# A two-layer hybrid decoder trunk on one NeuronCore: halved first weights, warm-up products, a shorter last norm, paired outputs, and a planner with longer notices

## The chip, the cores and the metric

The kernel runs on one core of a Trainium2 chip. The metric is the device time of one execution in microseconds (us). TensorE (PE) multiplies; a product is a weight load (PEld) and a stream of columns (a matmul) into a PSUM bank. VectorE (DVE), ScalarE (ACT) and GpSimd (POOL) do the rest; SyncE (SP) issues almost all DMAs.

## The reference

Input x is 1 x 1024 x 1024 in float32. Each of the two layers normalises, projects into four mixers, normalises each mixer's output, projects back and adds; then it runs a SwiGLU feed-forward network (FFN) with an inner width of 2816 and adds. A final norm ends it.

```python
for l in range(DEPTH):
    h = rmsnorm(x, attn_norm[l])
    proj = h @ w_in[l]
    ...
    y_a = mla_attention(...)          # latent attention, rotary keys, causal
    y_b = short_gated_conv(...)
    y_c = multiscale_pool(...)
    y_d = swa_sink_attention(...)     # sliding window of 128
    ...
    x = x + mixed @ w_o[l]
    h2 = rmsnorm(x, ffn_norm[l])
    gate, up = jnp.split(h2 @ w_gate_up[l], 2, axis=-1)
    x = x + (jax.nn.silu(gate) * up) @ w_down[l]
return rmsnorm(x, final_norm)
```

`rmsnorm` is x / sqrt(mean(x^2) + 1e-6) times a gain.

## The kernel before

*Layout.* x is held transposed: eight tiles of 128 features (`NK`), each in two halves t = 0, 1 of 512 positions (`HT`). All products run in fp32r, three per pair of tiles (`mm3`, L272): weights and activations are split into a rounded part `hi` and a remainder `lo`, and hi*hi, hi*lo and lo*hi are summed in PSUM. So every weight tile costs ACT a copy (L215 for the projections, L283 elsewhere) and DVE a subtraction (L216, L284), and every x tile that enters costs a gain copy on ACT (`act.activation(hi, f, AF.Copy, scale=gain)`, L286) and a subtraction on DVE (L287). The 2x2 block products of the FFN go through a Strassen-like scheme of seven products; the sums of the down weights that it needs are made on GpSimd (`dn_sums`, L161) and written to DRAM (`qd`).

*The start.* `par` (gains and other small constants, 128 x 86) is loaded on GpSimd's queue (L131), everything else on SP's. The first weights of the projections come through `weights` (L207: load of 128 x 1024; L215 copy; L216 subtraction), the x tiles through `enter` (L366), and their squares for the first norm through `SumSq.add` (L313 for the first square, L318 and L324 for a further square and its addition). The first products are those of the key weights with half 0 of x. `ones` is a 128 x 128 tile of ones, written by DVE at the start; a product with it sums over the partitions.

*The norm.* `SumSq.add` squares a tile on ACT and adds it to a running sum on DVE; the last addition also adds the epsilon (L320). `rnorm` multiplies the sum with `ones` (L336, in float32; L333 where the sum is split first), takes a logarithm and an exponential on ACT (L338, L339), refines the result (L340, L341, L344) and leaves 1/rms.

*The end.* In the last layer the last of the seven products of the down projection (`B22`) is done for columns 0 to 255 of half 1 first, then for 256 to 511: for each of four m, products into a bank, `evac` (L1575: adds the bank to x on DVE), squares. After the fourth, `rnorm(1, cols, tag="s")` and `finish`: for each of eight tiles one DVE instruction, x times gain times 1/rms (L380), and one output DMA of 128 x 256 (128 KB, L384). The output of half 0 leaves in 256 KB tiles.

*The order.* The program is recorded first; `order_engines` then sets the order of instructions on each engine. `steps_of` makes a step of each instruction with an estimated length; `arrange` runs a list schedule: each engine takes, of the steps whose inputs have arrived, the one with the smallest place. A place is the step's rank in the recorded program plus a number from the table `MOVES`, keyed by group (the neighbouring steps of one engine on one tile). `SIGNAL[a][b]` is the notice that engine b needs after a step of engine a ends; a PSUM bank or temporary may be taken anew 40 ns after its last use. In the trace each line number of a helper (L272, L283) stands for all its callers.

Of the kernel before, what the change touches and what calls it, by code (L numbers as in the profile page):

```python
# [18 lines left out]
P = 128  # L19
# [92 lines left out]
def trunk_kernel(ctx: ExitStack, tc: tile.TileContext, ins, out):  # L112
# [17 lines left out]
    par = cpool.tile([P, L * PC_N + NK], F32, name="par")  # L130
    pool.dma_start(par, ins["params"])  # L131
# [50 lines left out]

    def tmp(tag="te"):
        return tpool.tile([P, HT], F32, name=tag, tag=tag, bufs={"te": 2, "tn": 3, "tp": 3}[tag])
# [18 lines left out]
    def weights(src, n):  # L203
        if n > 2 * P:
            s = F.pair()
            raw = F.ap2(s)
            sp.dma_start(raw[:, :n], src)  # L207
# [7 lines left out]
        act.copy(hi[:, :n], raw[:, :n])  # L215
        dve.tensor_tensor(out=lo[:, :n], in0=raw[:, :n], in1=rd(hi[:, :n]), op=ALU.subtract)  # L216
# [20 lines left out]
    def expect_layer(l):  # L237
        for m in (2, 3, 0, 4, 5, 6, 1, 13, 14, 10, 11, 12, None, 7, 8, 9):
            if m is None:
                expect(rope_weights, l)  # L240
            else:
                expect(weights, ins["w_in"][l, m], 2 * HT)
        for d in range(NK):
            expect(weights, ins["w_o"][l, d, :, 2 * P :], 6 * P)
# [53 lines left out]
    class SumSq:  # L298
# [7 lines left out]
        def add(self, t, f, cols=whole):  # L306
# [12 lines left out]
            if m == self.n // P:  # L319
# [6 lines left out]
        def rnorm(self, t, cols=whole, tag="t", parts=False):  # L326
# [8 lines left out]
            else:  # L335
                pe.matmul(p, ones, a, start=True, stop=True)  # L336
# [24 lines left out]

    def enter(t):

        for k in range(NK):
            s = xf[k][t] = F.half()
            sp.dma_start(F.ap(s), x_in[k, :, t * HT : (t + 1) * HT])  # L366
            hh[k][t] = half_split(F.ap(s), pcol(0, PC_ATTN + k))

    def enter_norm(t):
# [3 lines left out]
        ratt[t] = ss.rnorm(t, parts=True)  # L373

# [10 lines left out]

    last_silu = None
    for l in range(L):
# [1251 lines left out]
        for cols in (slice(0, 256), slice(256, HT)) if last else ():  # L1639
            for m, p, w in tail:  # L1640
# [6 lines left out]
                ss.add(1, F.ap(x[2 * m][1])[:, cols], cols)  # L1647
            ratt[1] = ss.rnorm(1, cols, tag="s")
            finish(x, 1, cols)
# [6 lines left out]
    "DVE": {"PE": 55, "DVE": 33, "ACT": 33, "POOL": 79, "SP": 27},  # L1656
    "ACT": {"PE": 52, "DVE": 33, "ACT": 25, "POOL": 77, "SP": 26},
    "POOL": {"PE": 79, "DVE": 33, "ACT": 32, "POOL": 78, "SP": 27},
    "SP": {"PE": 50, "DVE": 35, "ACT": 35, "POOL": 80, "SP": 30},
}  # L1660
OVERLAP = {"DVE": 82, "ACT": 97, "POOL": 44}
# [43 lines left out]
DRAM_TILES = {"xs", "xp", "xr", "qd", "out"} | {f"ad{n}" for n in range(7)}  # L1705
# [112 lines left out]
def arrange(steps, rank=lambda v: v.rank):  # L1818
# [29 lines left out]
    def takes(v, t):  # L1848
        for name in (x for x in v.tiles if x not in live):
            tag = name.rsplit("_", 1)[0]  # L1850
            if queue[tag][0] != name or tag in held_by or not freed[tag] or freed[tag][0] + 40 > t:
                return False
        return True

    while any(now.values()) or any(later.values()):
# [23 lines left out]
        for name in (x for x in v.tiles if x not in live):  # L1879
# [5 lines left out]
            if freed[tag][0] + 40 > t:  # L1885
                wait = max(wait or 0, freed[tag][0] + 40)
# [284 lines left out]
```

## Time and profile before

| | us |
|---|---|
| median of 3 runs | 2055.86 (2055.63 to 2056.76) |
| the profiled execution, own time | 2055.69 |
| its span, first to last instruction | 2053.8 |
| PE busy | 2030.9 |
| mean granted clock of TensorE | 0.998 |
| HBM read / written | 204.66 MB / 83.36 MB |

The page's rows are groups of instructions: line, engine, operation, tile written <- tiles read, shape, count. In a timeline row the numbers are the start, the length from first start to last end, the engine and line, and in brackets the engine's idle time before it and what ended that. `SPq` rows are DMA issues. In the rows by stretch, each engine has its busy us and, in brackets, its count of instructions (PE, PEld, DVE, ACT, POOL), then PE's granted clock, the DMA share and GB/s. A waits row is: engine and what it made, who ended the wait, total us, times, longest us. A matmul's end is modelled and reaches past the start of the next one, so the pace is read from the starts.

### The profile page before, as it was taken

How to read it: one execution, taken by the hardware profiler on the slowest of the kernel's cores; microseconds unless marked ns; L12 is line 12 of the kernel's file. 1: busy time of each engine (PE TensorE's matmuls, PEld its weight loads, DVE VectorE, ACT ScalarE, POOL GpSimd, SP SyncE). 2: the span in 40 equal slices, each digit the busy share in tenths (PEclk: the TensorE clock that was granted, in tenths of full speed). 3: DMA queues.
4: the chain of work that ended last, by engine and by line, in shares of the span. 5: the costliest groups of instructions: out<-in, count | busy, mean ns of one | idle time of the engine just before them, and what ended most of it. 6: DMA issues, size and time to landing. Idle time of an engine off the chain costs nothing.

```text
span 2053.8 us, 26189 instructions
## 1 busy us (share of the span) xinstructions
PE 2030.9 (99%) x9394; PEld 1670.3 (81%) x9394; DVE 1616.5 (79%) x2696; ACT 991.6 (48%) x1738; POOL 203.5 (10%) x213
## 2 busy tenths in 40 slices
PE   8999999999999999999999999999999999999997
PEld 7887888878888888888888877878788888888887
DVE  7888989998877878655656898889987787786555
ACT  7447657653333335444433566667433333355342
POOL 0000000022222122000000000000222212120000
PEclk9999999999999999999999999999999999999999
DMA  5010222344544437856401102232553444497552
GB/s 182 34 52 31 77 91 95 129 144 170 180 144 171 166 139 263 297 207 210 149 22 54 47 24 93 81 121 80 185 186 137 161 177 143 153 320 266 200 176 85
DMA packets 148818, 289.75 MB, mean 141 GB/s; under 512 B 12608, under 2 KB 72000, under 8 KB 148688
## 3 DMA queue, kind: packets, MB, share of 16 engines
q1 hardware_dynamic: 148656, 288.03, 40.6%
q8 instruction: 74, 1.21, 0.2%
q14 instruction: 56, 0.46, 0.1%
q0 software_dynamic: 32, 0.04, 0.0%
HBM read 204.66 MB, written 83.36 MB: 140 GB/s over the span
## 4 chain that ended last, share of the span: by engine, by line
PE 72%; DVE 2%; ACT 2%; DMA 1%; POOL 0%; issue 0%; SPq 0%; DVEq 0%; ACTq 0%; POOLq 0%
PE ps_s L272 25%; PE ps_mm L272 25%; PE ps_t L272 10%; PE ps_pv L272 8%; PE ps_pv L962 1%; PE ps_t L950 1%; DMA ad<-u 1%; ACT u L283 0%; PE ps_s L896 0%; POOL u L161 0%; PE ps_t L336 0%; PE ps_s L897 0%; PE ps_s L898 0%; PE ps_s L511 0%; PE ps_mm L770 0%
## 5 line engine op out<-in xcount | busy, mean ns | idle before, releaser
L272 PE MATMUL ps_mm<-u,u 128*128 128x512 f32 (+1 forms) x3426 | 868.2, 390 | 2.6 <-ACT u L283 1.7
L272 PEld LDWEIGHTS ps_mm<-u,u 128*128 128x128 f32 x3426 | 627.5, 188 | 131.4 <-issue 5.0
L272 PE MATMUL ps_s<-u,u 128*128 128x512 f32 x2676 | 662.3, 391 | 8.0 <-ACT u L286 6.8
L272 PEld LDWEIGHTS ps_s<-u,u 128*128 128x128 f32 x2676 | 501.2, 188 | 117.1 <-ACT u L286 7.0
L283 ACT CAST u<-u 128x1024 fp32r<-128x1024 f32 (+2 forms) x388 | 336.4, 889 | 388.8 <-PE ps_s L272 83.8
L284 DVE TENSOR_TENSOR u<-u,u 128x1024 fp32r<-128x1024 f32 (+2 forms) x388 | 403.5, 1060 | 148.5 <-ACT u L283 124.0
L161 POOL TENSOR_TENSOR u<-u 128x256 f32<-128x256 f32 x176 | 196.0, 1116 | 759.0 <-DMA u<-in_w_dn 502.3
L272 PE MATMUL ps_t<-u,u 128*128 128x512 f32 (+1 forms) x1118 | 267.2, 378 | 0.0
L272 PEld LDWEIGHTS ps_t<-u,u 128*128 128x128 f32 x1118 | 202.2, 188 | 39.5 <-issue 0.5
L272 PE MATMUL ps_pv<-u,u 128*128 128x512 f32 x696 | 171.4, 390 | 0.0
L272 PEld LDWEIGHTS ps_pv<-u,u 128*128 128x128 f32 x696 | 130.5, 188 | 27.3 <-ACT tn L1176 0.2
L1316 ACT ACTIVATE tp<-tp 128x512 f32<-128x512 f32 x84 | 53.2, 633 | 155.4 <-DVE tp L348 154.9
L286 ACT ACTIVATE u<-u,par 128x512 fp32r<-128x512 f32 x100 | 69.6, 718 | 61.2 <-DVE u L1575 19.1
L959 POOL MEMSET u<- 128x128 f32 x32 | 6.6, 231 | 871.8 <-DVE u L652 622.0
L283 ACT CAST u<-ps_t 128x512 fp32r<-128x512 f32 (+4 forms) x136 | 64.7, 506 | 46.4 <-PE ps_t L950 29.4
L284 DVE TENSOR_TENSOR u<-ps_t,u 128x512 fp32r<-128x512 f32 (+4 forms) x136 | 76.3, 581 | 9.1 <-ACT u L283 8.5
L287 DVE SCALAR_TENSOR_TENSOR u<-u,par,u 128x512 fp32r<-128x512 f32 x100 | 72.7, 746 | 9.0 <-ACT u L286 8.9
L1317 DVE TENSOR_TENSOR tp<-tp,u 128x512 f32<-128x512 f32 x84 | 63.2, 753 | 20.3 <-ACT tp L1316 19.8
L1176 ACT COPY tn<-ps_s 128x512 f32<-128x512 f32 x66 | 38.4, 583 | 78.8 <-PE ps_s L272 78.7
L216 DVE TENSOR_TENSOR u<-u,u 128x1024 fp32r<-128x1024 f32 (+1 forms) x46 | 51.8, 1128 | 26.0 <-PE ps_t L272 12.3
L318 ACT ACTIVATE tn<-u 128x512 f32<-128x512 f32 (+1 forms) x93 | 52.7, 590 | 36.4 <-DVE u L1575 31.6
L348 DVE TENSOR_TENSOR tp<-tp,u 128x512 f32<-128x512 f32 x80 | 60.1, 751 | 1.6
(192 smaller groups left out, 2092.4 us busy)
## 6 DMA issues: line engine op xcount, KB each, us to landing
u<-in_w_gu SPq DMA_DIRECT2D x88, 512.0 KB, 3.6
ad<-u SPq DMA_DIRECT2D x154, 256.0 KB, 2.8
u<-ad SPq DMA_DIRECT2D x70, 512.0 KB, 5.4
u<-in_w_dn SPq DMA_DIRECT2D x68, 512.0 KB, 3.8
qd<-u SPq DMA_DIRECT2D x44, 512.0 KB, 3.0
u<-qd SPq DMA_DIRECT2D x32, 512.0 KB, 4.6
u<-in_w_in SPq DMA_DIRECT2D x30, 512.0 KB, 3.5
u<-in_xT SPq DMA_DIRECT2D x32, 256.0 KB, 4.1
```

What stands on the lines that cost most here:

```text
L161: pool.tensor_tensor(out=o, in0=o, in1=u, op=ALU.add)
L216: dve.tensor_tensor(out=lo[:, :n], in0=raw[:, :n], in1=rd(hi[:, :n]), op=ALU.subtract)
L272: pe.matmul(o, w, r, start=start and k == 0 and i == 0, stop=stop and k == n - 1 and i == 2, skip_group_check=again,)
L283: act.copy(hi, f)
L284: dve.tensor_tensor(out=lo, in0=f, in1=rd(hi), op=ALU.subtract)
L286: act.activation(hi, f, AF.Copy, scale=gain)
L287: dve.scalar_tensor_tensor(out=lo, in0=f, scalar=gain, in1=rd(hi), op0=ALU.mult, op1=ALU.subtract)
L318: act.activation(q, f, AF.Square)
L348: dve.tensor_tensor(out=o, in0=a, in1=b, op=ALU.mult)
L1176: act.copy(o, p)
L1316: last_silu = act.activation(g, g, AF.Silu)
L1317: dve.tensor_tensor(out=g, in0=g, in1=r, op=ALU.mult)
```

## The change

Five things are edited.

1. `par` becomes 128 x 128 (padded) and is loaded on SP's queue. The first weights (`w_in[0, 2]`) are loaded, copied and subtracted in two halves; between the issues of the two halves stand, in the recorded program, x tile 0 and `par` (`first_loads`). In the built order the two halves are issued one behind the other, then x tile 0, `par`, x tile 1.
2. `warm_up(8)`: eight float32 products of `ones` with `ones`, 128 columns each, into a bank whose content nobody reads, ahead of everything on PE.
3. In the last 256 columns, the squares of the last tile aren't added to the running sum: `rnorm` takes them as a second product with `ones` into the same bank (`also`); the epsilon is added one addition earlier (`closing`).
4. There too, the gain is multiplied onto each x tile on ACT as soon as the tile is complete (`gain`), the last multiplication is by 1/rms alone (`finish_gained`), and outputs leave in pairs of tiles (256 KB), but for the last pair, whose two tiles leave singly.
5. The planner: PE's notices from all other engines are 113 ns longer, a bank is taken anew by PE 153 ns after its last use (`REUSE`), and the table `MOVES` (490 entries before, 564 after) is another. The order of instructions is different on all engines.

The sums of the down weights stay on GpSimd. `"ws"` names a DRAM tile that the kernel doesn't have.

```diff
-    par = cpool.tile([P, L * PC_N + NK], F32, name="par")
-    pool.dma_start(par, ins["params"])
+    par = cpool.tile([P, P], F32, name="par")
...
+    def warm_up(n):
+        p = ps("pv")
+        for _ in range(n):
+            pe.matmul(p[:, :P], ones, ones, start=True, stop=True)
...
-    def weights(src, n):
+    def weights(src, n, between=None):
+        cuts = [slice(0, n // 2), slice(n // 2, n)] if between else [slice(0, n)]
...
-            sp.dma_start(raw[:, :n], src)
+            for c in cuts:
+                sp.dma_start(raw[:, c], src[:, c])
+                if c is not cuts[-1]:
+                    between()
...
-        act.copy(hi[:, :n], raw[:, :n])
-        dve.tensor_tensor(out=lo[:, :n], in0=raw[:, :n], in1=rd(hi[:, :n]), op=ALU.subtract)
+        for c in cuts:
+            act.copy(hi[:, c], raw[:, c])
+            dve.tensor_tensor(out=lo[:, c], in0=raw[:, c], in1=rd(hi[:, c]), op=ALU.subtract)
...
-            if m == self.n // P:
+            if m == self.n // P or closing:
...
-                pe.matmul(p, ones, a, start=True, stop=True)
+                pe.matmul(p, ones, a, start=True, stop=also is None)
+                if also is not None:
+                    pe.matmul(p, ones, also, start=False, stop=True)
...
+    def first_loads():
+        load_x(0, 0)
+        sp.dma_start(par, ins["params"])
...
+    def gain(x, d, t, cols):
+        a = F.ap(x[d][t])[:, cols]
+        act.activation(a, a, AF.Copy, scale=par[:, L * PC_N + d : L * PC_N + d + 1])
+
+    def finish_gained(x, t, cols):
+        r = F.ap(ratt[t])[:, cols]
+        sent = slice(t * HT + cols.start, t * HT + cols.stop)
+        for m in range(NK // 2):
+            o = F.ap2(F.pair()).rearrange("p (b n) -> p b n", b=2)[:, :, cols]
+            both = out[2 * m : 2 * m + 2, :, sent].rearrange("b p n -> p b n")
+            for b in range(2):
+                mul_to(o[:, b], F.ap(x[2 * m + b][t])[:, cols], r)
+                if m == NK // 2 - 1:
+                    sp.dma_start(both[:, b], o[:, b])
+            if m < NK // 2 - 1:
+                sp.dma_start(both, o)
...
+    warm_up(8)
...
-                ss.add(1, F.ap(x[2 * m][1])[:, cols], cols)
-            ratt[1] = ss.rnorm(1, cols, tag="s")
-            finish(x, 1, cols)
+                a = F.ap(x[2 * m][1])[:, cols]
+                if late and m == NM - 1:
+                    q = tmp("tn")[:, cols]
+                    act.activation(q, a, AF.Square)
+                else:
+                    ss.add(1, a, cols, late and m == NM - 2)
+                if late:
+                    for d in (2 * m, 2 * m + 1):
+                        gain(x, d, 1, cols)
+            ratt[1] = ss.rnorm(1, cols, tag="s", also=q)
+            (finish_gained if late else finish)(x, 1, cols)
...
-    "DVE": {"PE": 55, "DVE": 33, "ACT": 33, "POOL": 79, "SP": 27},
-    "ACT": {"PE": 52, "DVE": 33, "ACT": 25, "POOL": 77, "SP": 26},
-    "POOL": {"PE": 79, "DVE": 33, "ACT": 32, "POOL": 78, "SP": 27},
-    "SP": {"PE": 50, "DVE": 35, "ACT": 35, "POOL": 80, "SP": 30},
+    "DVE": {"PE": 168, "DVE": 33, "ACT": 33, "POOL": 79, "SP": 27},
+    "ACT": {"PE": 165, "DVE": 33, "ACT": 25, "POOL": 77, "SP": 26},
+    "POOL": {"PE": 192, "DVE": 33, "ACT": 32, "POOL": 78, "SP": 27},
+    "SP": {"PE": 163, "DVE": 35, "ACT": 35, "POOL": 80, "SP": 30},
 }
+REUSE = {"PE": 153, "DVE": 40, "ACT": 40, "POOL": 40, "SP": 40}
...
-            if freed[tag][0] + 40 > t:
-                wait = max(wait or 0, freed[tag][0] + 40)
+            if freed[tag][0] + REUSE[e] > t:
+                wait = max(wait or 0, freed[tag][0] + REUSE[e])
...
-    a["params"] = c(np.concatenate([lay.reshape(P, -1), fin], axis=1))
+    par = np.concatenate([lay.reshape(P, -1), fin], axis=1)
+    a["params"] = c(np.pad(par, ((0, 0), (0, P - par.shape[1]))))
```

More of the change, by code (lines that the diff above doesn't have):

```diff
@@ L241, in expect_layer @@
             else:
-                expect(weights, ins["w_in"][l, m], 2 * HT)
+                begin = [first_loads] if (l, m) == (0, 2) else []
+                expect(weights, ins["w_in"][l, m], 2 * HT, *begin)
         for d in range(NK):
@@ L304, in __init__, with add @@
             self.done = {}
-        def add(self, t, f, cols=whole):
+        def add(self, t, f, cols=whole, closing=False):
             e = EPS * self.n / P
@@ L324, in add, with rnorm @@
                 dve.tensor_tensor(out=a, in0=a, in1=q, op=ALU.add)
-        def rnorm(self, t, cols=whole, tag="t", parts=False):
+        def rnorm(self, t, cols=whole, tag="t", parts=False, also=None):
             a, n = F.ap(self.acc[t])[:, cols], self.n
@@ L360, in trunk_kernel, with load_x @@
     ratt = [None, None]
+    def load_x(k, t):
+        s = xf[k][t] = F.half()
+        sp.dma_start(F.ap(s), x_in[k, :, t * HT : (t + 1) * HT])
+    def first_loads():
+        load_x(0, 0)
+        sp.dma_start(par, ins["params"])
     def enter(t):
         for k in range(NK):
-            s = xf[k][t] = F.half()
-            sp.dma_start(F.ap(s), x_in[k, :, t * HT : (t + 1) * HT])
+            if (k, t) != (0, 0):
+                load_x(k, t)
+            s = xf[k][t]
             hh[k][t] = half_split(F.ap(s), pcol(0, PC_ATTN + k))
@@ L1639, in trunk_kernel @@
         for cols in (slice(0, 256), slice(256, HT)) if last else ():
+            late, q = cols.start > 0, None
             for m, p, w in tail:
@@ L1702, in areas @@
     return name, [(p, p + dims[0][1], c, c + span)]
-DRAM_TILES = {"xs", "xp", "xr", "qd", "out"} | {f"ad{n}" for n in range(7)}
+DRAM_TILES = {"ws", "xs", "xp", "xr", "qd", "out"} | {f"ad{n}" for n in range(7)}
 BUFS = {"ps_mm": 2, "ps_s": 3, "ps_t": 2, "ps_pv": 1, "te": 2, "tn": 3, "tp": 3, "vraw": 2, "vhi": 2, "vlo": 2, "sm1": 16, "sm2": 16, "sm16": 2}
@@ L1850, in takes @@
             tag = name.rsplit("_", 1)[0]
-            if queue[tag][0] != name or tag in held_by or not freed[tag] or freed[tag][0] + 40 > t:
+            if queue[tag][0] != name or tag in held_by or not freed[tag] or freed[tag][0] + REUSE[e] > t:
                 return False
```

123 rows, old and new, of the table MOVES are left out of this document.

## The prediction

> **What bounds the kernel now.** I read the page's shares first, then who PE and its weight loads wait for, then the two ends in the timeline and the chain of waits.
>
> ```profile
> span 2053.8 us, 26189 instructions
> PE 2030.9 (99%) x9394; PEld 1670.3 (81%) x9394; DVE 1616.5 (79%) x2696; ACT 991.6 (48%) x1738; POOL 203.5 (10%) x213
> ```
>
> TensorE is the bound: 22.9 us of the span pass without a product. The waits of PE and of its weight loads (waited for, total us, times, longest) say where:
>
> ```profile
> PE ps_s L272 <- ACT u L286: 6.8, 1, 6.8
> PE ps_mm L272 <- ACT u L283: 1.7, 2, 1.0
> PE ps_s L336 <- DVE u L320: 1.4, 1, 1.4
> PE ps_s L272 <- ACT u L283: 1.2, 2, 0.8
> ...
> PEld ps_s L272 <- ACT tn L1176: 3.4, 15, 0.3
> PEld ps_pv L962 <- ACT u L283: 3.0, 14, 0.3
> PEld ps_pv L962 <- DVE u L284: 2.0, 10, 0.2
> PEld ps_pv L572 <- ACT u L283: 2.0, 9, 0.3
> ```
>
> 6.85 us lie ahead of the first product. After the last product (it ends at 2044.53, below) come 9.3, and 1.42 just before it. 22.9 - 6.85 - 9.3 - 1.42 leaves 5.3 us in the middle. The rows on weight loads show more than that: a load that waits 0.2 us for a result that came just in time makes the product behind it late without PE counting as idle, because the modelled ends of the products cover it:
>
> ```profile
> 1337.90 0.48 PE L962 MATMUL ps_pv<-u,u 128*128 128x512 f32 x1
> 1338.21 0.28 PE L896 MATMUL ps_s<-u,u 128*128 128x256 f32 x1
> ...
> 700.00:800.00 100.00, 100.00 (x443) 82.83 (x442) 80.32 (x101) 37.74 (x51) 20.85 (x19) 1.00 0.50 172
> ```
>
> In the FFN stretch 443 products start in 100 us, 0.226 apart. The product of that width at 1337.90 has its successor 0.31 behind it: 0.085 us lost. So there are three places to win: head, middle, tail.
>
> **The head.** Before, the first weights land at 4.2, and the parameters (on GpSimd's queue, issued at 1.2) 4.8 us after their issue:
>
> ```profile
> L131 POOL DMA_DIRECT2D par<-in_params x1: 676/676/676, 1.2 to 1.2; - x1
> DMA to landing us min/median/max: 4.8/4.8/4.8
> ...
> 4.22 1.04 ACT L215 CAST u<-u 128x1024 fp32r<-128x1024 f32 x1 [2.21 <-DMA u<-in_w_in]
> 5.38 0.63 ACT L313 ACTIVATE u<-u 128x512 f32<-128x512 f32 x1
> 6.07 1.45 ACT L286 ACTIVATE u<-u,par 128x512 fp32r<-128x512 f32 x2
> 6.85 3.29 PE L272 MATMUL ps_s<-u,u 128*128 128x512 f32 x6 [6.85 <-ACT u L286]
> ```
>
> 1.2 + 4.8 = 6.0: the gain copy (L286) at 6.07 waited for the parameters, and the first product for that copy. The change sends the parameters on SP's queue, fourth, behind the two halves of the weights and the first x tile (0.42 us of SP's time for each issue, by the next rows). SP then issues the second x tile a DMA or two later than before. That matters: in the built order ScalarE squares x tile 0, then x tile 1, and only then makes the gain copy of tile 0, where before it made both copies first. So the first product now waits for tile 1, not for the parameters. Before, two x tiles took 4.2 and 5.1 us to land (issued at 1.2 and 1.6: 5.4 and 6.7).
>
> ```profile
> L366 SPq DMA_DIRECT2D u<-in_xT x2: 421/422/424, 1.2 to 1.6; - x2
> DMA to landing us min/median/max: 4.2/4.7/5.1
> ```
>
> As many bytes go ahead of tile 1 as before, without GpSimd's queue among them: I take 5.7 as its landing, between 5.2 and 6.8. Then a square (0.63) and a copy (0.72, half of 1.45) set the first product at 7.0 (6.5 to 8.1), against 6.85. The halved weights bring nothing here: both halves are copied (0.6 each) before tile 1 is in.
>
> The warm-up is about these rows:
>
> ```profile
> 11.21 2.10 PE L272 MATMUL ps_mm<-u,u 128*128 128x512 f32 x5
> 13.15 0.63 PE L272 MATMUL ps_s<-u,u 128*128 128x512 f32 x2
> ...
> 2029.10 0.61 PE L336 MATMUL ps_s<-u,ones 128*128 128x256 f32 x2
> 2043.83 0.70 PE L336 MATMUL ps_s<-u,ones 128*128 128x256 f32 x2 [1.42 <-DVE u L320]
> 2047.00:2048.00 1.00, 0.00 (x0) 0.00 (x0) 1.00 (x3) 0.00 (x0) 0.00 (x0) 0.62 0.00 0
> 2048.00:2049.00 1.00, 0.00 (x0) 0.00 (x0) 1.00 (x4) 0.00 (x0) 0.00 (x0) 0.50 0.60 207
> ```
>
> Early products start 0.427 apart (five cover 2.10 less the last one's tail), later ones 0.23: until about 12.9 us PE runs at half pace. Some 14 products (6.3 us from 6.85 to 13.15, less a short wait, at 0.427) lose 0.2 each, 2.8 us. A ones product of 256 columns takes two passes of 0.21; one of 128 columns costs 0.21, at half pace 0.43, so eight take 3.4 us, from about 1.1, when the engines have started, to 4.5. They use time in which PE idles, so they cost nothing. Do they help? The granted clock at the end fell to a half at about 2047.2 (0.62 in that microsecond), 2.7 us after the last product. From 4.5 to 7.0 is a pause of 2.5 us, as good as that one, so I take the warm clock as lost again or never reached: no gain. Bounds: 2.8 us gained if it holds, 1.5 lost if the first product comes at 8.1 and the clock rises as late as now. I take 0.
>
> [...]
>
> **The tail.** The chain after the last evacuation:
>
> ```profile
> 2042.90 0.42 ACT tn L318
> 2043.34 0.44 DVE u L320
> 2043.83 0.71 PE ps_s L336 x2
> ...
> 2046.92 0.48 DVE u L380
> ...
> L384 SPq DMA_DIRECT2D out<-u x8: 332/396/405, 2047.4 to 2050.8; - x8
> DMA to landing us min/median/max: 1.7/1.8/1.9
> ```
>
> The last squares go straight into the ones product: the add L320 and its hand-over (2043.34 to 2043.83, less 0.03) leave the chain, 0.46 us. The product of the older sum runs while the squares are made. The gains move to ScalarE, which idles there; the last lies beside the ones product (0.42 beside 0.71). If it did not, it would add 0.42. So the multiplications start at 2046.46. A three-operand product with the gain took 0.48; plain tensor_tensor of that shape 0.425:
>
> ```profile
> L380 DVE SCALAR_TENSOR_TENSOR u<-u,par,u 128x256 f32<-128x256 f32 x8 | 3.3, 481 | 0.0
> L324 DVE TENSOR_TENSOR u<-u,tn 128x256 f32<-128x256 f32 x3 | 1.3, 425 | 1.0 <-ACT tn L318 1.0
> ```
>
> Eight at 0.41 (3.3 / 8) take 3.3; with 0.055 less each, 2.85: done at 2049.3, not 2050.2. Before, SP was behind: eight issues from 2047.4 to 2050.8, 0.49 apart, the last landing at 2052.6. Now there are five, and the built order puts the two single tiles first and the three pairs last, so the last is a 256 KB pair at 2049.4. First-half outputs of 256 KB, alone on the queue, landed in 2.1:
>
> ```profile
> L384 SPq DMA_DIRECT2D out<-u x3: 332/337/338, 2019.4 to 2020.7; - x3
> DMA to landing us min/median/max: 2.0/2.1/2.1
> ```
>
> 2049.4 + 2.1 to 2.3 (the pair has 1 KB rows) is 2051.5 to 2051.7: 1.0 us earlier (0.5 to 1.2).
>
> **The middle.** The planner's notice from every engine to PE grows by 0.113 us, its re-use of a PSUM bank by PE from 0.040 to 0.153, and the list of moves is new: no arithmetic is added, but the order on every engine is another. What the order alone tells: I took each product that uses a result of ScalarE or VectorE and counted PE's work, at the pitches above, back to the product from which that result descends, less the copies and subtractions between. Before, 39 products stand within 0.1 us of their earliest start, after 2. Each costs about 0.085, so 37 are 3.1 us. The four rows of weight loads above count 48 short waits, the rest of that view about as many, a hundred in all; so some 60 more than the 39 are late through ACT's and DVE's queues, not through data; a notice longer by 0.113 should cover a third of them, 20 x 0.085 = 1.7. I count nothing for the long waits (1.7 + 1.2 + 0.7 us above), which are late weight copies. Sum 4.8 us. Bounds: 100 x 0.085 and the 5.3 of idle, 13.8 gained; and 6 lost (below).
>
> **Sum.** The profiled execution took 2055.69 us (span 2053.8, 1.9 around it), 0.17 under the median 2055.86. 2055.69 - 0 - 1.0 - 4.8 = 2049.9.
>
> **Rivals.**
> *The warm clock holds.* For: eight products are 3.4 us of work. Against: the 2.5 us pause beside the 2.7 that closed it. 2049.9 - 2.8 = 2047.1.
> *The order only moves the waits.* For: copies queue for DVE, which is busy 94% where PE waits most (below), whatever PE does. Against: 39 tight products against 2. Middle 0: 2055.69 - 1.0 = 2054.7.
> *VectorE becomes the bound of the attention stretches.*
>
> ```profile
> 300.00:400.00 100.00, 99.80 (x490) 81.58 (x489) 94.04 (x192) 69.08 (x140) 1.07 (x6) 1.00 0.36 125
> 400.00:500.00 100.00, 99.20 (x434) 80.52 (x433) 93.57 (x128) 51.41 (x75) 22.49 (x20) 1.00 0.42 145
> ...
> 1400.00:1500.00 100.00, 97.88 (x426) 79.08 (x425) 94.40 (x136) 57.27 (x87) 17.43 (x16) 1.00 0.39 135
> ```
>
> In these three DVE idles 18 us of 300. A planner that passes over nearly ready products hands DVE its input later by up to 0.113; 53 of the 456 instructions there passing it on make 6 us, and with 18 us that had other reasons nothing absorbs them: 2055.69 - 1.0 + 6 = 2060.7. It decides from about 45. Against: DVE does not gain work, and PE's other products are there to fill.
>
> **How the numbers follow.** Forecast 0.52, clock holds 0.10, waits moved 0.23, DVE bound 0.15. 0.2% is 4.1 us, about what a measurement of this kernel tells from no change: faster below 2051.75, slower above 2059.97. The forecast's own range is 2047.0 to 2052.5 (middle 2 to 8), some 0.06 of its 0.52 above 2051.75: faster 0.46 + 0.10 + 0.02 of the moved waits = 0.58; slower 0.13; same 0.29. The range reaches down to 2045.0 (the held clock with a middle of 7) and up to 2056.5, past the moved waits with the head's loss; left out is mostly the DVE rival.
>
> **What would show it.** Head: the first real product near 7.0 behind a square and a gain copy, 0.427 spacing after it; at 0.227 from its start the clock held. Tail: no DVE add before the last ones product, multiplications 0.35 apart, five output DMAs, the last about 2 us before the end. Middle: fewer weight-load waits of 0.2 us on L283, L284 and L1176, and PE's count per 100 us up in 100 to 500 and 1100 to 1500. I am wrong if these waits stay as many, or if DVE's idle time in the three stretches grows.

## The result, and the profile after

| | before | after |
|---|---|---|
| median (22 runs each, same chip) | 2056.19 us (2054.15 to 2057.89) | 2052.65 us (2051.68 to 2054.97) |
| span of the profiled execution | 2053.8 us | 2050.5 us |
| mean granted clock | 0.998 | 0.999 |

The ratio is 0.9984, with a 95% interval of 0.9977 to 0.9990: between 2 and 5 us faster. The forecast was 2049.9. The time lies 2.8 above it: inside the whole range of 2045.0 to 2056.5, but just above the forecast's own (2047.0 to 2052.5) and above 2051.75, the line below which I had called it faster. Of the 2.8, 0.5 lies in the kernel before, whose median over 22 runs is 2056.19, where the prediction starts from 2055.69.

In the kernel after, line numbers moved: the `hi` copies and subtractions are L294 and L295 (before L283, L284), the gain copies L297 and L298, the squares L324 and L329, the projections' weight copies L225 and L226, `mm3` L283, the ones products L344, L347, L349, `evac` L1615, the warm-up L186.

First the shares on the page, and who PE waited for (waited for, total us, times, longest), in the whole span:

```profile
span 2050.5 us, 26241 instructions
PE 2030.1 (99%) x9412; PEld 1676.1 (82%) x9412; DVE 1611.3 (79%) x2696; ACT 994.5 (49%) x1747; POOL 205.8 (10%) x212
...
PE ps_mm L283 <- ACT u L297: 4.0, 1, 4.0
PE ps_pv L344 <- DVE u L295: 1.4, 1, 1.4
PE ps_t L283 <- DVE u L295: 1.1, 2, 0.6
...
PE ps_s L283 <- ACT u L294: 0.9, 1, 0.9
...
PE ps_s L349 <- ACT tn L1691: 0.5, 1, 0.5
```

The 1.42 us ahead of the last ones product became 0.5 (L349). The wait at the start is 4.0 between warm-up and first product. The long waits in the middle (L344, L283) reach 1.4 us, where before they reached 1.0. The next rows are the waits of weight loads (PEld) from 60 to 2000 us, those on the lines that the prediction named (L294 and L295 are its L283 and L284, L1002 its L962, L612 its L572):

```profile
...
PEld ps_s L283 <- ACT u L294: 2.1, 4, 1.4
PEld ps_t L283 <- DVE u L295: 1.9, 2, 1.0
PEld ps_pv L344 <- DVE u L295: 1.8, 1, 1.8
...
PEld ps_pv L1002 <- DVE u L295: 1.6, 8, 0.3
...
PEld ps_pv L612 <- ACT u L294: 0.8, 3, 0.5
...
PEld ps_pv L1002 <- ACT u L294: 0.2, 1, 0.2
```

Most short waits on ScalarE are gone: the 14 waits of 3.0 us on its copies are one of 0.2, the 9 of 2.0 are three of 0.8, and the row on L1176 (15 times, now L1216) has vanished. The short waits on VectorE's subtractions hardly moved: the 10 of 2.0 us are 8 of 1.6. Rows with few and long waits now stand near the top.

The head, from the timeline (start, length, group, idle time before and what ended it):

```profile
1.05 3.79 PE L186 MATMUL ps_pv<-ones 128*128 128x128 f32 x16 [1.05 <-DVE ones L134]
...
6.75 0.63 ACT L324 ACTIVATE u<-u 128x512 f32<-128x512 f32 x1 [1.65 <-DMA u<-in_xT]
7.59 0.63 ACT L329 ACTIVATE tn<-u 128x512 f32<-128x512 f32 x1 [0.22 <-DMA u<-in_xT]
8.13 3.77 ACT L297 ACTIVATE u<-u,par 128x512 fp32r<-128x512 f32 x6
8.88 5.00 PE L283 MATMUL ps_mm<-u,u 128*128 128x512 f32 x10 [4.05 <-ACT u L297]
```

Square of tile 0, square of tile 1, then the gain copy, then the first product at 8.9: the order was as forecast, the times were not. Tile 0 landed at 6.7, tile 1 at 7.6. Ten products lie in 5.00 us, half pace, until 13.9 (12.9 before).

The tail, from the timeline, and the pairs' issues with their time to landing:

```profile
2040.56 0.42 DVE L1615 TENSOR_TENSOR u<-u,ps_mm 128x256 f32<-128x256 f32 x1 [2.63 <-PE ps_mm L283]
2041.01 0.42 ACT L1691 ACTIVATE tn<-u 128x256 f32<-128x256 f32 x1 [3.00 <-DVE u L1615]
2041.46 0.51 ACT L399 ACTIVATE u<-u,par 128x256 f32<-128x256 f32 x1
2041.48 0.70 PE L349 MATMUL ps_s<-tn,ones 128*128 128x256 f32 x2 [0.53 <-ACT tn L1691]
...
2044.52 2.77 DVE L361 TENSOR_TENSOR u<-u,u 128x256 f32<-128x256 f32 x8
...
L412 SPq DMA_DIRECT2D out<-u x3: 372/382/382, 2046.0 to 2047.3; - x3
...
DMA to landing us min/median/max: 2.1/2.1/2.2
```

No add stands between the squares and the ones product, the gain (L399) lies beside that product, and the last pair lands at 2047.3 + 2.1 = 2049.4. From the last evacuation to the last landing that is 8.9 us; before it was 10.2 (evacuation at 2042.44, landing at 2052.6).

So the span's 3.3 us are: tail 1.3 won; head lost (12 products started by 14.05 us where before had 18; six at 0.227 are 1.4); and the middle 3.4 won, as what is left.

### The profile page after: what moved, and what is told of

It is laid out like the page before. It is cut to its first block, busy times and chain, and to the rows that moved or that the text cites. A ratio compares the mean times of both kernels' runs of the same rounds, so it can differ in the third digit from the quotient of the medians.

```text
span 2050.5 us, 26241 instructions
## 1 busy us (share of the span) xinstructions
PE 2030.1 (99%) x9412; PEld 1676.1 (82%) x9412; DVE 1611.3 (79%) x2696; ACT 994.5 (49%) x1747; POOL 205.8 (10%) x212
## 4 chain that ended last, share of the span: by engine, by line
PE 89%; DVE 7%; ACT 1%; DMA 1%; issue 1%; POOL 0%; SPq 0%; DVEq 0%; ACTq 0%; POOLq 0%
PE ps_mm L283 35%; PE ps_s L283 27%; PE ps_t L283 10%; PE ps_pv L283 8%; PE ps_pv L1002 2%; DVE u L295 1%; PE ps_t L990 1%; PE ps_t L347 1%; PE ps_s L936 1%; PE ps_s L937 1%; PE ps_s L938 1%; PE ps_mm L810 1%; DVE u L298 1%; PE ps_pv L612 1%; PE ps_s L551 1%
## 5 line engine op out<-in xcount | busy, mean ns | idle before, releaser
L283 PE MATMUL ps_mm<-u,u 128*128 128x512 f32 (+1 forms) x3426 | 874.1, 389 | 5.6 <-ACT u L297 4.0
L283 PEld LDWEIGHTS ps_mm<-u,u 128*128 128x128 f32 x3426 | 628.7, 188 | 135.7 <-ACT u L297 4.3
L283 PE MATMUL ps_s<-u,u 128*128 128x512 f32 x2676 | 661.2, 390 | 1.5 <-ACT u L294 0.9
L283 PEld LDWEIGHTS ps_s<-u,u 128*128 128x128 f32 x2676 | 501.4, 188 | 108.1 <-ACT u L294 2.1
L294 ACT CAST u<-u 128x1024 fp32r<-128x1024 f32 (+2 forms) x388 | 336.1, 889 | 416.6 <-PE ps_s L283 83.4
L295 DVE TENSOR_TENSOR u<-u,u 128x1024 fp32r<-128x1024 f32 (+2 forms) x388 | 401.6, 1054 | 151.3 <-ACT u L294 119.4
L283 PE MATMUL ps_t<-u,u 128*128 128x512 f32 (+1 forms) x1118 | 275.2, 377 | 1.1 <-DVE u L295 1.1
L283 PEld LDWEIGHTS ps_t<-u,u 128*128 128x128 f32 x1118 | 202.5, 188 | 40.3 <-DVE u L295 1.9
L283 PE MATMUL ps_pv<-u,u 128*128 128x512 f32 x696 | 170.9, 389 | 0.0
L283 PEld LDWEIGHTS ps_pv<-u,u 128*128 128x128 f32 x696 | 130.6, 188 | 27.2
L297 ACT ACTIVATE u<-u,par 128x512 fp32r<-128x512 f32 x100 | 69.6, 718 | 52.4 <-DVE u L1139 15.5
L294 ACT CAST u<-ps_t 128x512 fp32r<-128x512 f32 (+4 forms) x136 | 64.8, 507 | 52.6 <-PE ps_t L990 35.9
L295 DVE TENSOR_TENSOR u<-ps_t,u 128x512 fp32r<-128x512 f32 (+4 forms) x136 | 76.4, 583 | 8.7 <-ACT u L294 8.0
L298 DVE SCALAR_TENSOR_TENSOR u<-u,par,u 128x512 fp32r<-128x512 f32 x100 | 73.1, 748 | 12.3 <-ACT u L297 12.2
L226 DVE TENSOR_TENSOR u<-u,u 128x1024 fp32r<-128x1024 f32 (+2 forms) x47 | 52.1, 1108 | 25.8 <-ACT u L225 16.8
L1216 ACT COPY tn<-ps_s 128x512 f32<-128x512 f32 x66 | 38.4, 582 | 67.3 <-PE ps_s L283 67.3
L329 ACT ACTIVATE tn<-u 128x512 f32<-128x512 f32 (+1 forms) x92 | 52.6, 591 | 28.6 <-DVE u L1615 25.6
```

Source lines behind the costliest of these rows:

```text
L226: dve.tensor_tensor(out=lo[:, c], in0=raw[:, c], in1=rd(hi[:, c]), op=ALU.subtract)
L283: pe.matmul(o, w, r, start=start and k == 0 and i == 0, stop=stop and k == n - 1 and i == 2, skip_group_check=again,)
L294: act.copy(hi, f)
L295: dve.tensor_tensor(out=lo, in0=f, in1=rd(hi), op=ALU.subtract)
L298: dve.scalar_tensor_tensor(out=lo, in0=f, scalar=gain, in1=rd(hi), op0=ALU.mult, op1=ALU.subtract)
L329: act.activation(q, f, AF.Square)
```

## The experiments

All but two of the kernels (those without moves) hold the changed kernel's planned order as a list and alter only what is named, so that nothing else moves. They ran in three groups of four, each on one chip with runs of the kernel before (medians 2055.62, 2055.42 and 2055.59).

| kernel | median us (runs) | ratio to before (95%) |
|---|---|---|
| old tail | 2055.32 (11) | 0.9996 (0.9988 to 1.0005) |
| old head | 2051.81 (11) | 0.9979 (0.9970 to 0.9988) |
| 22 warm-up products | 2050.57 (7) | 0.9971 (0.9960 to 0.9982) |
| old order in the middle | 2060.13 (11) | 1.0018 (1.0009 to 1.0027) |
| changed kernel again | 2052.70 (11) | 0.9989 (0.9980 to 0.9998) |
| gain copy first | 2050.98 (11) | 0.9983 (0.9975 to 0.9992) |
| gain copy first, 18 products | 2049.17 (8) | 0.9971 (0.9961 to 0.9981) |
| that, x tile 0 between the halves | 2051.07 (11) | 0.9981 (0.9972 to 0.9990) |
| no moves, old notices | 2076.84 (4) | 1.0112 (1.0098 to 1.0127) |
| no moves, new notices | 2082.90 (4) | 1.0136 (1.0122 to 1.0149) |
| single outputs | 2052.85 (10) | 0.9986 (0.9977 to 0.9995) |
| best, second version | 2047.96 (5) | 0.9966 (0.9952 to 0.9979) |

Intervals are some 2 us wide to each side, so differences of 1 us are read from the traces, stage by stage.

**Old tail.**

```diff
-            late, q = cols.start > 0, None
+            late, q = False, None
```

> The changed kernel with its planned order kept instruction by instruction, and only the last half's norm and output put back as before: a last add on VectorE, one product of ones, multiplications with the gain, eight single outputs. From the start of the last evacuation to the last landing the trace of the kernel before has 10.2 us, that of the changed one 8.9. My theory, that this stretch ends the span and nothing covers it: 1.3 to 1.5 us slower than the changed kernel, about 2054.0 where that has 2052.6, and the stretch again at 10.0 to 10.3. The rival, that the last outputs' landing is set by the transfers and not by the work ahead of them: no difference, 2052.6.

Measured: 2055.3, that is 1.4 to 2.5 us above the changed kernel by the two ratios of that. Its timeline and its single outputs' issues:

```profile
2041.21 0.42 DVE L1615 TENSOR_TENSOR u<-u,ps_mm 128x256 f32<-128x256 f32 x1 [2.57 <-PE ps_mm L283]
...
2042.17 0.42 DVE L331 SCALAR_TENSOR_TENSOR u<-tn,u 128x256 f32<-128x256 f32 x1 [0.54 <-ACT tn L329]
...
2045.75 3.26 DVE L419 SCALAR_TENSOR_TENSOR u<-u,par,u 128x256 f32<-128x256 f32 x8
...
L423 SPq DMA_DIRECT2D out<-u x24: 332/402/1442, 2017.4 to 2049.7; - x24
```

The last issue at 2049.7 landed 1.9 later: 10.3 us after the last evacuation. The stretch is 1.4 longer than 8.9 with everything ahead of it the same. The theory held; the rival would have kept 8.9.

**Old head.** Gains on GpSimd's queue, whole weights, no warm-up, before's order up to 40 us.

```diff
-    par = cpool.tile([P, P], F32, name="par")
+    par = cpool.tile([P, L * PC_N + NK], F32, name="par")
+    pool.dma_start(par, ins["params"])
...
-        cuts = [slice(0, n // 2), slice(n // 2, n)] if between else [slice(0, n)]
+        cuts = [slice(0, n)]
...
-    warm_up(8)
```

> The changed kernel with the head of before (gains by GpSimd's queue, whole first weights, no warm-up product, and before's order up to 40 us), and the changed kernel's order and tail after it. In the changed kernel's trace the first product starts at 8.9 us and the clock opens at 13.9, in that of before at 6.8 and 12.9. My theory, that the changed head costs what these two times say and nothing later takes it back: 1.2 to 1.8 us faster than the changed kernel, about 2051.1. The rival, that the load of x tile 0 landed late (6.7 against 5.4) only in that one profiled execution: no difference, 2052.6, and a first product near 6.8 in profiles of kernels with the changed head.

Measured: 2051.8; the ratio cannot be told from the changed kernel's. The first product came at 6.7. But in the nine profiles that load in the changed order x tile 0 landed at 5.3 to 6.1 in eight, at 6.7 in one, and the first product, with the copy behind the squares, came at 7.8 to 8.4 in five and at 8.9 in that one. So the late tile 0 was that execution's own, as the rival has it, but in the others too the first product is 1.0 to 1.5 us later than before (6.8): neither theory nor rival. Where the two orders meet, at 44 us, TensorE stood 0.8 us, so the time says little; the run is inconclusive, the landing times are not.

**22 warm-up products.**

```diff
-    warm_up(8)
+    warm_up(22)
```

> The changed kernel, order kept, with 22 warm-up products instead of 8. At the pace of the trace (0.427 us each while the clock is at half) they run from 1.05 to 7.1 us and, if the clock opens there, to 8.8, where the first product is due. My theory, that the pause from 4.6 to 8.9 kept the clock at half until 13.9: the clock opens near 7.1, products are 0.227 instead of 0.427 us apart from the first, and the run is 2.0 to 2.5 us faster than the changed kernel, about 2050.3. The rival, that the first products wait for tiles of x and not for the clock: under 0.7 us faster, 2052.0 or more. A third: if products that run on into 9 us only push the first ones back, it is slower, by up to 0.5 us.

Measured: 2050.6. By stretch (busy us and count of PE, PEld, DVE, ACT, POOL; granted clock; DMA share; GB/s), first this kernel, then the kernel before. The clock column shows 1.00 also where the trace has no clock record yet; there the pace tells:

```profile
4.50:6.00 1.50, 1.50 (x15) 1.50 (x15) 1.17 (x4) 0.80 (x2) 0.00 (x0) 1.00 0.95 318
...
10.00:12.00 2.00, 2.00 (x10) 1.68 (x9) 2.00 (x4) 2.00 (x4) 0.00 (x0) 1.00 1.02 386
```

```profile
10.00:12.00 2.00, 2.00 (x6) 1.58 (x5) 2.00 (x4) 2.00 (x5) 0.00 (x0) 1.00 1.04 390
```

15 passes in 1.5 us are 0.1 apart, where the eight products of the changed kernel (two passes each) took 0.21 a pass throughout: the clock opened at 4.2 and stayed open; ten products between 10 and 12 us for six. 23 products had started by 14.05 us. By 35 us it was 2.6 us ahead of the changed kernel's first profile, a little more than expected, but only 1.5 ahead of the second. The gain is real, my size for it was taken from an execution with a late start.

**Old order in the middle.** The order of before between 40 us and the last half.

```diff
   order on every engine: the changed kernel's up to 40 us,
-    the changed kernel's from there on
+    that of before from there on,
+    the changed kernel's in the last half
```

> The changed kernel's instructions and its order up to 40 us and in the last half, with the order of before from 40 us on in between. Between the traces of before and after the middle is 3.4 us shorter. My theory, that the longer notices in the planner made that gain by turning short stops of TensorE into none: 2.8 to 4.0 us slower than the changed kernel, about 2056.0, with TensorE's waits with a named releaser back from 67 to some 105 between 20 and 2024 us. The rival, that the order is worth nothing and the 3.4 us are differences of one execution: within 1 us, 2052.6.

Measured: 2060.1, by the ratios 6 to 7 us above the changed kernel, more than expected. I counted for each pair of neighbouring products how far apart they start beyond the usual pitch of such a pair (its 5th percentile over the traces), from 60 to 2000 us, and the waits of weight loads for which the profile names what ended them:

```
kernel               15 to 250 ns     over 250 ns     waits of loads
before               267, 19.4 us     24, 11.8 us     107, 31.7 us
old order            255, 18.5        24, 13.5        103, 32.0
changed              214, 14.6        31, 15.5         64, 23.2
changed again        209, 15.0        34, 17.4         67, 25.8
best, second         202, 13.7        29, 14.6         56, 20.8
```

In this profile and that of before two rows stand near the top, of which the changed order lacks the first and has the second once:

```profile
PEld ps_s L283 <- ACT tn L1216: 3.4, 15, 0.3
PEld ps_pv L1002 <- ACT u L294: 2.9, 13, 0.3
```

The waits go with the order, not with the execution: all ten profiles with the changed order have 56 to 68, both with the old one more than 100. Of the excess 2.9 us belong to my cuts: by the same count TensorE lost 2.1 and 2.9 us around the two joints (14 to 60, 2000 to 2034), the changed kernel 0.5 and 1.6. The 3 to 4 us that are left for the order agree with the 3.4 between the first two profiles.

**The changed kernel again.**

> The changed kernel with its planned order written down, nothing else: a second profiled execution, to be set beside the three of this call. Four profiles of kernels with the changed loads have x tile 0 landing at 6.7, 5.5, 6.1 and 5.5 us, and three of them the full clock for one stretch of 3.4 us during the warm-up products. My theory, that the late first product of the changed kernel's first profile (8.9 us) was that execution's own: x tile 0 at 5.4 to 6.1, first product at 7.7 to 8.4, and 18 products started by 14.05 us as in the kernel before (11 in the first profile). The rival, that it belongs to the change: first product at 8.7 or later, 11 to 13 products by 14.05.

Measured: 2052.7. Tile 0 landed at 5.8, tile 1 at 6.8, first product at 8.2, 16 products by 14.05 (12 in the first profile; the 11 of the expectation left out one at 14.03). The theory held but for its 18. (Of the three kernels that the expectation counts with the full clock, the one with 22 products kept it.) The clock in this execution, by stretch:

```profile
5.57:8.98 3.41, 0.53 (x2) 0.22 (x2) 1.94 (x8) 2.74 (x5) 0.00 (x0) 1.00 0.98 334
8.98:12.40 3.42, 3.42 (x8) 2.74 (x9) 3.42 (x6) 3.42 (x6) 0.00 (x0) 0.50 1.06 402
12.40:14.05 1.65, 1.65 (x8) 1.35 (x8) 1.65 (x3) 1.65 (x4) 0.00 (x0) 1.00 1.00 412
```

It was open from 5.6 to 9.0, when PE had almost nothing to do, and at half for the next 3.4 us, when it had. Further down this execution lost what it had won at the head: it ends 0.9 behind. Of that 1.0 is one stop near 1346 us, behind a load of output weights:

```profile
PE ps_mm L283 <- ACT u L225: 1.0, 1, 1.0
...
1345.91 0.83 ACT L225 CAST u<-u 128x768 fp32r<-128x768 f32 x1 [2.31 <-DMA u<-in_w_o]
```

That load took 5.5 us to land here, 4.2 in the first profile (no stop). In the nine profiles with the changed order and the load in its place it took 4.0 to 4.6 in four (a stop of at most 0.2) and 5.1 to 5.5 in five (0.6 to 1.0).

**Gain copy first.**

```diff
   ScalarE: copy w half 1, copy w half 2,
+    gain copy x0,
     square x0, square x1,
-    gain copy x0,
     gain copy x1, ...
```

> The changed kernel, order kept, but ScalarE makes the gain copy of x tile 0 before the squares of tiles 0 and 1, and VectorE its remainder before the first add. In three profiles the first product comes 2.2 to 2.4 us after the landing of x tile 0, with both squares and the landing of x tile 1 between. My theory, that the copy behind the squares sets the first product: it starts 0.8 us after x tile 0 has landed, 1.4 us sooner, and the run is 0.4 to 1.4 us faster than the changed kernel (less than 1.4 since products are at half clock until 11.5 to 14 us and the later tiles land 0.65 apart). The rival, that later tiles of x set the pace from the second product on: the first product is as early, the run within 0.3 us of the changed kernel.

Measured: 2051.0, 1.7 below the changed kernel on the same chip, a little more than expected; the first product at 6.6 against 8.2, 20 products by 14.05 against 16:

```profile
5.79 0.72 ACT L297 ACTIVATE u<-u,par 128x512 fp32r<-128x512 f32 x1 [0.96 <-DMA par<-in_params]
...
6.57 0.50 PE L283 MATMUL ps_mm<-u,u 128*128 128x512 f32 x1 [1.73 <-ACT u L297]
```

The theory on the order held, but the product came 1.2 after tile 0's landing (5.4), not 0.8: the copy now waits for the gains (5.7), which stand behind tile 0 on SP's queue.

**Gain copy first and 18 warm-up products.**

> The gain copy first as in the run before, and 18 warm-up products, which at the traces' pace (0.427 us each at half clock, 0.214 at full clock) end between 6.5 and 7.5 us, where the first product is due. My theory, that the long warm-up (1.1 us of gain against an ordinary start of the changed kernel, from 23 products by 14.05 us against 18) and the earlier copy add up: 1.8 to 2.8 us faster than the changed kernel, about 2050.0. The rival, that at full clock the products wait for the tiles of x (0.65 us apart, three products of 0.227 each): no faster than the long warm-up alone, 1.0 to 1.5 us.

Measured: 2049.2, ratio 0.9971 against 0.9989 for the changed kernel on the same chip: 3.5 us by the medians, more than theory or rival said; 23 products by 14.05. The first product came at 7.05, right behind the last warm-up pass (7.02). By 14.05 it had started as many as with 22 warm-up products and no earlier copy, so for the head the rival is right: from then on the tiles of x set the pace (from 7 to 14 us weight loads waited 2.0 us for gain copies and their remainders, L297 and L298). The seven products more than in the changed kernel's second profile are 1.6 us; the load near 1340, which landed early in this profile, is 1.0.

**That, with x tile 0 between the halves.**

```diff
   SyncE: w half 1,
+    x0, gains,
     w half 2,
-    x0, gains,
     x1, ...
```

> The kernel of the run before, with x tile 0 and the gains loaded between the halves of the first weights, as the program text has them, and not behind both. In the traces each 256 KB behind another lands 0.65 us later. My theory: x tile 0 lands 0.65 us sooner, the first product starts as much sooner, and the run is 0.2 to 0.6 us faster than the run before. The rival, that the fifth tile's products then wait for the second half's split or that tiles of x set the pace: no difference.

Here the gain copy of x tile 0 also stands ahead of the copy of the second half on ScalarE.

Measured: 2051.1, 1.9 above the run before; a miss. Tile 0 landed at 4.2, but the warm-up held PE until 6.9, and the second half of the weights came at 7.1:

```profile
4.57 0.72 ACT L297 ACTIVATE u<-u,par 128x512 fp32r<-128x512 f32 x1 [0.38 <-DMA par<-in_params]
...
7.17 0.62 ACT L225 CAST u<-u 128x512 fp32r<-128x512 f32 x1 [1.88 <-DMA u<-in_w_in]
```

The rival's wait is there (20 products by 14.05 for 23, that is 0.7 us); about 0.8 more is the stop near 1346.

**No moves, old and new notices.** The table of moves empty, the notices of before or of after.

```diff
-MOVES = {...}
+MOVES = {}
```

> The changed program with the notices of before and no hand-written moves at all (the table of moves empty), to be set beside the next run, so that the notices are the only difference. In the profiles so far, between 60 and 2000 us, kernels with before's order have 145 and 150 weight loads of TensorE that waited (42.4 us in all), those with the changed order 103 to 115 (33 to 37 us). Both theories: some 20 to 40 us slower than the changed kernel, since the moves are missing. My theory: 145 or more waits of weight loads here.

> The same with the longer notices and still no moves. My theory, that the notices themselves keep products away from what they wait for: waits of weight loads fall by a third or more against the run before, most of it among stops of 15 to 250 ns, while stops over 250 ns grow; for the time I give no sign, between 8 us faster and 8 us slower than the run before. The rival, that the moves were fitted anew and the notices as such do nothing: as many waits as in the run before, within 10%.

Measured: 2076.8 and 2082.9. Waits of weight loads, counted as in the expectation, 159 and 105, those with a named end 114 and 58; stops of 15 to 100 ns 237 (15.0 us) and 185 (12.6); stops over 250 ns 39 (27.3) and 49 (37.1). The longer notices by themselves, with the later re-use of banks, do what was said of short waits, and pay with long ones. Without fitted moves they win no time, so the gain of the middle is not theirs alone; the old notices with the new moves were not run. The 6 us between the two have one more cause, TensorE's clock. In the kernel with new notices it was at half in seven stretches of 3.41 us behind the head, in that with old ones in two; here one of the seven with the stretch ahead of it, in which PE stood 1.58 us for a copy on ScalarE (busy us and count of PE, clock, DMA share, GB/s):

```profile
228.24:231.65 3.41, 1.77 (x9) 1.00 0.08 32
231.65:235.06 3.41, 3.41 (x13) 0.50 0.11 38
```

From 60 to 2000 us, products in stretches at half clock lost about 9 us beyond their usual pitch with the new notices and 1.5 with the old ones. That is nearly 8 of the 10 us by which the two profiles differ in this count. At full clock stops of 15 to 250 ns fell from about 22 to 16 us, and those over 250 ns grew from 27 to 36. The clock also tells the runs of the old notices apart: three took 2076.5 to 2077.0 at a mean clock of 0.995 to 0.996, the fourth 2083.3 at 0.994, as slow as those with the new notices (0.993 to 0.994). In the changed kernel and that of before no stretch between 14 us and the last products is at half.

**Single outputs.**

```diff
             for b in range(2):
                 mul_to(o[:, b], F.ap(x[2 * m + b][t])[:, cols], r)
-                if m == NK // 2 - 1:
-                    sp.dma_start(both[:, b], o[:, b])
-            if m < NK // 2 - 1:
-                sp.dma_start(both, o)
+                sp.dma_start(both[:, b], o[:, b])
```

> The changed kernel with its last half's outputs sent one tile at a time, eight transfers for five. The multiplications come 0.336 us apart in the changed kernel's trace, single outputs 0.49 us apart in that of before. My theory, that the issuing queue then sets the pace: from the last evacuation to the last landing 9.5 to 9.8 us against 8.9, so about 0.8 us of the tail's gain hangs on the pairs. The rival, that the last multiplication sets the end: 8.6 (a single output lands 0.3 us faster than a pair, 1.8 against 2.1), a little better than pairs.

```profile
2038.48 0.42 DVE L1612 TENSOR_TENSOR u<-u,ps_mm 128x256 f32<-128x256 f32 x1 [2.63 <-PE ps_mm L283]
...
2042.89 3.81 SPq L409 DMA_DIRECT2D out<-u  x8
...
DMA to landing us min/median/max: 1.8/1.9/1.9
```

Eight issues, 0.49 apart, from 2042.9 to 2046.3, the last landing at 2048.2: 9.7 us after the evacuation, for 8.9. SyncE's queue sets the pace, and 0.8 of the tail's 1.4 are the pairs. The time (2052.9) can't show it: the executions differ by 3 us.

**Best, second version.**

```diff
   SyncE, at two places:
+    output weights (768 columns),
     reload, reload,
-    output weights (768 columns),
   SyncE, at the end:
-    single, single, pair, pair, pair
+    pair, pair, pair, single, single
```

> The best kernel so far (copy first, 18 warm-up products), with two orders changed. First, at two places the load of output weights goes ahead of the two reloads that it stands behind on SyncE's queue; in the profiles it lands 4.1 to 5.5 us after its issue near 1340 us, and where it took 5.4 or more TensorE stood for 1.0 us. Second, the last outputs are sent pairs first and single tiles last. My theory: no stop near 1346 us (at most 0.2), and from the last evacuation to the last landing 8.6 us for 8.9; in the time 0.3 to 1.3 us faster than the best so far, about 2048.5. The rival, that the reloads then land later and TensorE waits for these instead, and that the last landing goes by the last multiplication: no difference, 2049.2.

Measured: 2048.0, the best of all, 7.6 below the kernel before; against the first best version (2049.2, on another chip) the intervals overlap. Near 1340 the load landed in 3.5 us and ScalarE did not wait for it; the stop behind it is gone, and so is one of 0.5 us that the first best version had at the other place, near 331 us:

```profile
1341.36 0.84 ACT L225 CAST u<-u 128x768 fp32r<-128x768 f32 x1
```

Long stops did not grow elsewhere (29 over 250 ns in both), so the rival's later reloads cost nothing that shows. The tail did not get shorter: 9.0 for the 8.9. The last single was issued only 0.55 after the one before it, at 2043.04 with the last multiplication done at 2042.67.

## Why the prediction was right, and where it was off

*Tail: right, a little small.* Forecast 1.0 (0.5 to 1.2), measured 1.3 on the last stretch, 1.4 with the old tail put back, just above my upper bound. The add left the chain, the gains hid beside the ones product, the multiplications are 0.336 apart where I had taken 0.35. The last pair landed in 2.1, the low end of my 2.1 to 2.3.

*Head: the order was right, one landing was mis-sized.* The step that failed is "I take 5.7 as its landing", for x tile 1. It landed between 6.2 and 7.6 in nine profiles (6.8 before): as many bytes stood ahead of it as before and it came about as late, and I had taken a microsecond off for GpSimd's queue. A square and a copy behind it gave, as forecast, 1.3 us more: first products at 7.8 to 8.4 and once 8.9, where I had 7.0 (6.5 to 8.1). The price is less than the delay: two products of 0.227 at most in ordinary executions, 1.4 us in the one profiled first. I had counted 0 with a bound of 1.5.

*Warm-up: right, for both reasons given.* "Lost again or never reached": in five of the profiles with eight products the clock opened for one stretch of 3.4 us and closed, so that at most the first few products ran at full clock and the next ones at half; in three it did not open. The pause was not the 2.5 us that I had reckoned with but 3.0 to 4.1 in the changed order, as the first product came later; with the gain copy first it was 1.7, and the clock closed all the same. With 18 or 22 products it opened in all four and stayed. The clock changed at another moment in each execution: it opened for good at 13.9 in the first profile of the changed kernel, at 12.4 in its second and at 12.9 in the kernel before.

*Middle: one term right, one left out.* The 4.8 us were for 57 short stops of 0.085 us each. Stops of 15 to 250 ns became 53 fewer (58 in the second profile) and fell from 19.4 to 14.6 us (15.0), by 4.4 to 4.8: right in number and in size, though it is the waits on ScalarE that went and hardly those on VectorE. What failed is the step "I count nothing for the long waits": stops over 250 ns grew from 11.8 to 15.5 and 17.4. That a scheduler which holds a product back by 0.113 does other work first, and runs out of it later, would explain this; the runs without moves show the exchange, not this reason for it. Between 14 and 2034 us all time beyond the usual pitch went from 47.9 to 46.0, 1.9 of the 3.4; the remaining 1.5 the counts do not resolve. In the second profile the middle won only 1.4, half of the difference for the late load near 1340; there short and long stops together are 32.4 us, for 31.2 in the kernel before, so that the counts do not resolve these 1.4 at all. That the order makes the gain is shown by putting the old one back; that short stops make it is shown only in part. So the rival "the order only moves the waits" was half true, and its 2054.7 is no farther from the measured time than the forecast. Of the 2.8 us above the forecast, 0.5 is the kernel before's own. The first profile lies 2.4 above, by 1.4 in the middle and 1.4 at the head, less 0.3 at the tail; in ordinary starts the head's share is at most 0.5 and the middle's the greater.

*VectorE as the bound: did not happen.* Its idle time in the three stretches went from 18 to 15 us:

```profile
300.00:400.00 100.00, 98.53 (x485) 80.84 (x484) 92.64 (x189) 69.32 (x139) 1.07 (x6) 1.00 0.35 123
400.00:500.00 100.00, 98.47 (x432) 80.36 (x431) 94.83 (x131) 52.32 (x78) 25.67 (x20) 1.00 0.41 143
...
1400.00:1500.00 100.00, 99.06 (x436) 80.99 (x435) 97.48 (x139) 58.50 (x88) 19.16 (x16) 1.00 0.40 139
```

PE's count in these three hardly moved (1350 to 1353). The sign that I had named for a gain, more products per 100 us from 100 to 500 and from 1100 to 1500, was there, if small: 3771 before, 3795 after, with more in six of the eight stretches. From 1200 to 1300 (before, then after):

```profile
1200.00:1300.00 100.00, 99.41 (x473) 79.32 (x472) 88.00 (x197) 61.95 (x139) 1.49 (x8) 1.00 0.21 71
```

```profile
1200.00:1300.00 100.00, 99.77 (x481) 80.97 (x481) 91.59 (x204) 65.72 (x146) 1.05 (x6) 1.00 0.21 70
```

## What to carry to other kernels

Here a scheduler's longer notice spared short waits and paid with long ones: count both, by length, in the traces of before and after, and for more than one execution. A warm-up helped here only where it lasted until the first real product; one that ended 1.7 to 4.1 us ahead of it did not hold the clock. Look at what stands ahead of the first product on each engine and on the issuing queue: moving one copy ahead of two squares brought that product 1.6 us forward.

## What the hardware showed that I had not expected

The clock also closed behind stretches in which PE had worked. In the kernel without moves and with new notices it was at half right after stretches of 3.41 us in which PE was busy for 1.06 to 1.77 us, so with up to half the stretch at work; in the one with old notices it was still open after one with 1.59. So in these profiles the busy time of a stretch alone does not tell whether the clock closes. Nor does it tell whether it opens: the eight warm-up products took 3.79 us in the changed kernel's first profile, where the clock stayed at half until 13.9, and as good as the same in its second, where it was open from 5.6 to 9.0:

```profile
1.05 3.78 PE L186 MATMUL ps_pv<-ones 128*128 128x128 f32 x16 [1.05 <-DVE ones L134]
```

With eight products it opened for such a stretch in five profiles of eight. What made the difference is not shown here.

One and the same load, from the same place of the queue, took 4.0 to 5.5 us to land in nine profiles. In the two of the changed kernel, with nothing changed between them, it took 4.2 and 5.5, and that decided about 1 us of the time.
